# Moving weight sums out of the second down phase, and one operation for the last norm

## The chip, the cores and the metric

One core of a Trainium2 chip (trn2) runs the whole kernel. The metric is the device time of one execution in microseconds (us); smaller is better. TensorE (PE) multiplies, VectorE (DVE) and ScalarE (ACT) work on tiles element by element, GpSimd (POOL) and SyncE (SP) mostly issue DMA transfers.

## The reference, cut to what matters

```python
def swiglu(h, w_gate, w_up, w_down):
    return (jax.nn.silu(h @ w_gate) * (h @ w_up)) @ w_down

def reference(x, ...):                       # x: 1024 tokens x 1024 features, float32
    x = x + 0.5 * swiglu(rmsnorm(x, ffn1_norm), ffn1_w_gate, ffn1_w_up, ffn1_w_down)
    x = x + hybrid_mixer(rmsnorm(x, mix_norm), ...)
    x = x + 0.5 * swiglu(rmsnorm(x, ffn2_norm), ffn2_w_gate, ffn2_w_up, ffn2_w_down)
    return rmsnorm(x, final_norm)            # x / sqrt(mean(x*x) + eps) * final_norm
```

The hidden width is 2816, which is 22 blocks of 128 rows. The change concerns the second `swiglu` and the last `rmsnorm`.

## The kernel before

**Products.** Every float32 operand is cut into a rounded high part (`fp32r`, made by ACT, line 169) and the rest (DVE, line 170); a product is three matmuls, high by high, high by low, low by high. The large products go by a scheme of seven products on 2 x 2 blocks instead of eight: sums and differences of the blocks on either side are multiplied (P1, P2, P3, P5, P6, P7, Q4), and the seven results are added up into four output blocks. All matmuls are recorded on line 91.

**Phases.** `gate_up(i)` computes the hidden activations of FFN number i (0 for the first, 1 for the second), one hidden block m per unit, and `down(i)` multiplies them by the down weights. The mixer lies between `down(0)` and `gate_up(1)`. `down` runs sixteen turns over four output groups g (`TURNS`, line 376). A turn takes two or three row pairs q of the eleven (`NQ`): turn 0 two, turns 1 to 12 three, turns 13 to 15 two, so a turn is 42 or 63 matmuls. Turns 0 to 11 add their partial results in DRAM with an accumulating DMA (`Turn.add`, line 835, issued by POOL); turns 12 to 15 finish the outputs in SBUF (`Turn.end`, line 875) and call `ready`, which for i = 1 is `to_output`: sum of squares on ACT (line 1382), mean on DVE (1385, 1388), product with the weights `gb` of the norm on DVE (1390), the power -1/2 on POOL (1395), the product with it on DVE for one half (1399) and on ACT for the other (1401), and the store (1402).

**Where the sums of the down phase come from.** The two phases are built differently.
- In `down(0)` the stationary operand is made of the weights. `left` (line 460) takes four raw weight blocks from the prefetching loader `L` (two buffers, so loads run two turns ahead), makes three sums on DVE (lines 482, 484, 485) and splits seven operands. The moving operand is hidden activations: `Aside` made their sums during `gate_up(0)` and put all seven away in DRAM (`c_sp[0]`, line 644); `rights_back` (line 748) reads them back, four loads ahead.
- In `down(1)` the stationary operand is hidden activations. `Aside` put the seven sums away in `c_sp[1]`; `left_back` (line 503) reads them back straight into `w` tiles, each load issued just ahead of its split. The moving operand is weights: `rights_rows` (line 764) takes a 1 MB raw row pair from `L`, makes four sums on DVE (line 771) and splits seven operands.

**Order.** The tile framework keeps each engine's instructions in one queue, in an order that it works out when the kernel is built; a waiting instruction holds up those behind it. `MADE` and `UPTO` (lines 374, 375) say how many moving operands must be ready after each turn, in both phases. P1 and P2 of a turn share a PSUM bank, as do P7 and Q4, and P5 and P3: the second may start only when the first has been read out (lines 842 and 845 for P1, 858 for P7, 860 for P5). `s` tiles come from a pool of 72 buffers, `w` tiles from one of 10.

Of the kernel before, what the change touches and what calls it, by code (L numbers as in the profile page):

```python
# [10 lines left out]
F32 = mybir.dt.float32  # L11
# [6 lines left out]
P = 128  # L18
# [7 lines left out]
HALF = 512  # L26
# [15 lines left out]
def hybrid_block(ctx: ExitStack, tc: tile.TileContext, t: dict):  # L42
# [329 lines left out]


# [10 lines left out]
    def ffn_weights(i, pre, nstd):  # L384
# [6 lines left out]
        for j, (g, q0, q1) in enumerate(TURNS):  # L391
            if i:
                continue
            n = (q1 - q0) * P
            rows = wd[2 * q0 * P : 2 * q1 * P].rearrange("(k two p) c -> two p k c", two=2, p=P)
            yield [(b * n, n, (lambda a: a.rearrange("p (k c) -> p k c", c=P)),
                    rows[two, :, :, d * P : (d + 1) * P])
                   for b, (two, d) in enumerate(((1, g), (0, g), (1, g + 4), (0, g + 4)))]
        for q in range(NQ * i):
            yield [part(0, wd[2 * q * P : 2 * (q + 1) * P])]  # L400

# [101 lines left out]
    def left_back(g, q0, q1):  # L503

        a = {}
        n = (q1 - q0) * P

        def load(to, i):
            nc.sync.dma_start(out=to.rearrange("p (k c) -> p k c", c=P),
                              in_=c_sp[1][i, q0:q1, :, g * P : (g + 1) * P].rearrange("k p c -> p k c"))  # L510

        def begin(i):
            raw = w4(F32)[:, : 2 * n]
            for j in range(2):
                load(raw[:, j * n : (j + 1) * n], i + j)
            return raw

        yield a
        raw = begin(0)
        yield  # L520
        for i, after_it in ((0, 4), (4, 2), (2, 6)):
            now = raw
            if after_it < 6:
                raw = begin(after_it)
            else:
                raw = s()[:, :n]
                load(raw, 6)
            parts = split(w4()[:, : 2 * n], w4()[:, : 2 * n], now)
            for j in range(2):
                a[FACTORS[i + j]] = tuple(x[:, j * n : (j + 1) * n] for x in parts)  # L530
            yield
        a["Q4"] = split(s(F32R)[:, :n], s(F32R)[:, :n], raw)
        yield

# [97 lines left out]

    class Aside:

        def __init__(self, i):
            self.sp, self.op = c_sp[i], ALU.add if i else ALU.subtract
            self.names = (("P1", "P5", "P2", "P3", "P7", "P6", "Q4"), ("P1", "P7", "P2", "Q4", "P5", "P6", "P3"))[i]
            self.raw = 0, 2, 3, (1 if i else None)  # L640
            self.even = {}

        def put(self, j, i, x):
            nc.gpsimd.dma_start(out=self.sp[FACTORS.index(self.names[i]), j], in_=x)  # L644
# [4 lines left out]

        def take(self, m, hf, x):  # L650
            j, odd = divmod(m, 2)
            if not odd:
# [3 lines left out]
                else:  # L656
                    self.e1 = x
                    self.t1 = self.comb(s(), self.e0, x, self.op)
# [4 lines left out]
            else:  # L663
# [3 lines left out]
                t3 = self.comb(self.e1, x, self.e1, self.op)  # L667
                self.put(j, 4, t3)
                t4 = self.comb(s(), t2, self.o0, self.op)
# [5 lines left out]
    def gate_up(i, act, started, nstd):  # L675
# [50 lines left out]
        for m in range(nstd + 2, NF):  # L726
# [4 lines left out]
            else:  # L731
                prep = iter(())
                makers[i] = Prep(i)
                makers[i].begin(0)
            for n, name in enumerate(FEW):
                unit.do(name)
                next(prep, None)
                if i in makers:
                    makers[i].step()
                    makers[i].upto(UPTO[0] * (n + 1))  # L740
# [7 lines left out]
    def rights_back(ahead=4):  # L748
# [4 lines left out]
        def load():  # L753
            q, name = todo[len(raws)]
            raws.append(s())
            nc.sync.dma_start(out=raws[-1], in_=c_sp[0][FACTORS.index(name), q])
# [7 lines left out]
    def rights_rows():  # L764


        def done(name, x):
            b[name] = split(s(F32R), s(F32R), x)

        def comb(out, x, y, op):  # L770
            nc.vector.tensor_tensor(out=out, in0=x, in1=y, op=op)  # L771
            return out

        for q in range(NQ):
            b = ring[q] = {}
            raw, _ = L.take()
            b11, b12, b21, b22 = (raw[:, i * HALF : (i + 1) * HALF] for i in range(4))
            done("P1", b11)
            comb(b11, b11, b12, ALU.subtract)
            yield  # L780
            done("P7", comb(b12, b22, b12, ALU.subtract))
            yield
            done("P5", b11)
            yield
            done("P6", comb(b11, b11, b22, ALU.add))
            yield
            done("P2", b21)
            comb(b21, b11, b21, ALU.subtract)
            yield
            done("Q4", b21)  # L790
            yield
            done("P3", b22)
            L.load()
            yield

    class Prep:


        def __init__(self, i):
            self.i, self.made, self.lefts = i, 0, iter(())  # L800
            self.rights = rights_rows() if i else rights_back()
# [6 lines left out]
        def begin(self, j):  # L808
            if j < len(TURNS):
                g, q0, q1 = TURNS[j]  # L810
                self.lefts = left_back(g, q0, q1) if self.i else left(L.take()[0], (q1 - q0) * P, "P3")
# [564 lines left out]
    def to_output(tt, hf):  # L1376
# [13 lines left out]
        nc.vector.tensor_tensor(out=r, in0=r, in1=gb[hf], op=ALU.mult)  # L1390
# [5 lines left out]
        for hf in range(2):  # L1396
            r = rows[tt, hf]
            if hf:
                nc.vector.tensor_scalar(out=r, in0=r, scalar1=inv, scalar2=None, op0=ALU.mult)
            else:  # L1400
                nc.scalar.activation(r, r, AF.Identity, scale=inv)
# [29 lines left out]
```

## Time and profile before

| | us |
|---|---|
| median of 3 runs | 1896.9 (1896.22 to 1897.58) |
| the profiled execution | 1896.36 |
| its span, first to last instruction | 1894.7 |
| mean granted TensorE clock | 0.986 of full |

PE is busy for 97% of the span, DVE for 73%, ACT for 47%, POOL for 13%. The span is about: first `gate_up` to 476 us, `down(0)` to 689, mixer to about 1240, second `gate_up` to 1643, `down(1)` to 1886, then the last outputs. A time is read against PE: where PE is busy at full clock, other engines cost nothing; where it isn't, the rows say what it waited for.

### The profile page before, as it was taken

The numbers are of one execution on the slowest core, as the hardware profiler recorded it, in microseconds if no ns is written. First come the engines' busy times: TensorE is split into PE (matmuls) and PEld (weight loads), VectorE is DVE, ScalarE is ACT, GpSimd is POOL, SyncE is SP. The second block draws the span as 40 slices with busy tenths as digits, with TensorE's granted clock in tenths as the row PEclk, the third lists the DMA queues.
The fourth block names the chain that finished last, engine by engine and source line by source line (L and its number), as shares of the span: only waits on it lengthen the run. The fifth ranks groups of instructions, "written<-read, shape, count | busy, mean of one in ns | idle before, by whom it ended". The sixth has DMA issues, their size and how long they took to land.

```text
span 1894.7 us, 23205 instructions
## 1 busy us (share of the span) xinstructions
PE 1833.0 (97%) x8200; PEld 1508.1 (80%) x8200; DVE 1381.2 (73%) x2167; ACT 893.5 (47%) x1602; POOL 252.4 (13%) x400
## 2 busy tenths in 40 slices
PE   6999999999999999999999999999999999989997
PEld 5777888888888878888888878887888888777775
DVE  4788666666777797768787898658766666755768
ACT  3543222223555455667677775524322222344544
POOL 1201101010222221010101000210110101122211
PEclk8999999999999999999999999999999999999998
DMA  7213333334999853241313343412433333598985
GB/s 235 93 56 127 102 106 106 109 97 143 239 232 223 229 195 91 63 100 34 95 45 73 98 136 103 145 47 60 149 107 111 100 98 104 174 196 207 211 192 180
DMA packets 252933, 246.93 MB, mean 130 GB/s; under 512 B 14176, under 2 KB 197008, under 8 KB 252816
## 3 DMA queue, kind: packets, MB, share of 16 engines
q1 hardware_dynamic: 217072, 157.87, 27.8%
q0 software_dynamic: 35744, 87.58, 18.3%
q8 instruction: 64, 1.05, 0.2%
q14 instruction: 53, 0.43, 0.1%
HBM read 150.76 MB, written 85.20 MB: 125 GB/s over the span
## 4 chain that ended last, share of the span: by engine, by line
PE 68%; issue 15%; DVE 7%; DMA 4%; POOL 3%; ACT 1%; SPq 1%; POOLq 0%; DVEq 0%; ACTq 0%
PE ps L91 67%; DMA w<-c_sp 2%; DVE w L170 1%; DVE s L875 1%; POOL r_sp L835 1%; POOL c_sp L644 1%; DVE s L170 1%; DMA s<-c_sp 1%; DVE s L269 1%; PE ps L277 0%; DVE s L176 0%; POOL x_sp L835 0%; ACT w L169 0%; DMA r_sp<-s 0%; DMA raw<-in_ffn_w_gate 0%
## 5 line engine op out<-in xcount | busy, mean ns | idle before, releaser
L91 PE MATMUL ps<-s,w 128*128 128x512 f32 (+1 forms) x6400 | 1527.1, 393 | 38.6 <-ACT s L175 11.8
L91 PEld LDWEIGHTS ps<-s,w 128*128 128x128 f32 x6400 | 1198.2, 189 | 293.7 <-ACT s L175 12.7
L169 ACT CAST w<-raw 128x1024 fp32r<-128x1024 f32 (+2 forms) x158 | 157.5, 998 | 289.1 <-PE ps L91 189.1
L170 DVE TENSOR_TENSOR w<-raw,w 128x1024 fp32r<-128x1024 f32 (+2 forms) x158 | 182.0, 1153 | 109.4 <-PE ps L91 56.0
L91 PE MATMUL ps<-s,s 128*128 128x512 f32 (+3 forms) x944 | 241.4, 382 | 6.0 <-ACT s L858 4.3
L91 PEld LDWEIGHTS ps<-s,s 128*128 128x128 f32 x944 | 177.7, 189 | 46.1 <-ACT s L858 6.5
L644 POOL DMA_DIRECT2D c_sp<-s x154 | 83.5, 542 | 763.1 <-DVE s L630 579.8
L170 DVE TENSOR_TENSOR w<-w,w 128x768 fp32r<-128x768 f32 (+2 forms) x102 | 103.3, 1013 | 78.5 <-ACT w L169 39.3
L170 DVE TENSOR_TENSOR s<-s,s 128x512 fp32r<-128x512 f32 (+2 forms) x181 | 118.6, 670 | 39.8 <-ACT s L169 39.2
L169 ACT CAST w<-w 128x768 fp32r<-128x768 f32 (+2 forms) x102 | 89.6, 878 | 85.1 <-DMA w<-c_sp 39.3
L169 ACT CAST s<-s 128x512 fp32r<-128x512 f32 (+2 forms) x181 | 104.6, 607 | 43.4 <-DMA s<-c_sp 31.6
L626 ACT ACTIVATE s<-s 128x512 f32<-128x512 f32 x38 | 24.1, 633 | 190.0 <-DVE s L625 190.0
L170 DVE TENSOR_TENSOR s<-raw,s 128x512 fp32r<-128x512 f32 (+2 forms) x131 | 86.2, 666 | 25.9 <-ACT s L169 25.5
L482 DVE TENSOR_TENSOR w<-raw 128x1024 f32<-128x1024 f32 (+2 forms) x54 | 60.6, 1124 | 47.7 <-PE ps L91 46.7
L169 ACT CAST s<-raw 128x512 fp32r<-128x512 f32 (+2 forms) x131 | 76.7, 602 | 38.7 <-DVE raw L771 38.6
L611 ACT ACTIVATE s<-ps 128x512 f32<-128x512 f32 x38 | 22.7, 598 | 113.2 <-PE ps L91 113.2
L1254 DVE TENSOR_TENSOR s<-s,ps 128x128 f32<-128x128 f32 (+2 forms) x96 | 52.7, 548 | 16.8 <-ACT s L1250 16.4
L1242 ACT ACTIVATE s<-ps 128x128 f32<-128x128 f32 (+2 forms) x96 | 47.0, 490 | 37.7 <-PE ps L91 37.3
L835 POOL DMA_DIRECT2D r_sp<-s x48 | 41.6, 876 | 149.6 <-ACT s L854 48.3
L1250 ACT ACTIVATE s<-s 128x128 f32<-128x128 f32 (+2 forms) x96 | 50.2, 523 | 20.6 <-DVE s L1246 19.3
L617 DVE TENSOR_TENSOR s<-s,ps 128x512 f32<-128x512 f32 x38 | 26.0, 685 | 45.0 <-PE ps L91 45.0
L835 POOL DMA_DIRECT2D x_sp<-s x48 | 41.6, 866 | 126.3 <-DVE s L860 60.6
(133 smaller groups left out, 1697.6 us busy)
## 6 DMA issues: line engine op xcount, KB each, us to landing
c_sp<-s POOLq DMA_DIRECT2D x154, 256.0 KB, 2.5
raw<-in_ffn_w_gate SPq DMA_DIRECT2D x43, 512.0 KB, 3.9
raw<-in_ffn_w_up SPq DMA_DIRECT2D x43, 512.0 KB, 5.2
x_sp<-s POOLq DMA_DIRECT2D x80, 256.0 KB, 4.5
s<-c_sp SPq DMA_DIRECT2D x77, 256.0 KB, 7.1
r_sp<-s POOLq DMA_DIRECT2D x64, 256.0 KB, 5.1
w<-c_sp SPq DMA_DIRECT2D x72, 192.0 KB, 5.0
raw<-in_ffn_w_down SPq DMA_DIRECT2D x11, 1024.0 KB, 8.9
```

The costliest lines, as they stand in the source:

```text
L91: nc.tensor.matmul(out, lhs, rhs, **kw)
L169: nc.scalar.copy(hi, x)
L170: nc.vector.tensor_tensor(out=lo, in0=x, in1=f(hi), op=ALU.subtract)
L482: nc.vector.tensor_tensor(out=two(y), in0=two(blk(1, 2)), in1=blk(3).unsqueeze(1).to_broadcast([P, 2, n]), op=ALU.add)
L611: last_silu[0] = nc.scalar.activation(self.s0, o, AF.Silu)
L617: nc.vector.tensor_tensor(out=self.u3, in0=self.u2, in1=self.o[2], op=ALU.add)
L626: last_silu[0] = nc.scalar.activation(self.u2, self.u2, AF.Silu)
L644: nc.gpsimd.dma_start(out=self.sp[FACTORS.index(self.names[i]), j], in_=x)
L835: nc.gpsimd.dma_start(out=self.acc(self.g + 4 * i, hf), in_=x, accum_op=ALU.add)
L1242: behind(nc.scalar.activation(u["s"][:, cols], u["z"][:, cols], AF.Exp), table_set)
L1250: nc.scalar.activation(sc, sc, AF.Ln, bias=1.0)
L1254: nc.vector.tensor_tensor(out=sc, in0=sc, in1=u["z"][:, cols], op=ALU.max)
```

## The change

`down(1)` gets the form of `down(0)`. `Aside` for i = 1 no longer makes sums of the hidden activations: each hidden tile goes as it is to a new DRAM tensor `l_sp`, in four pieces per row, and the loader `L` reads four blocks of it per turn for `left`. During `gate_up(1)` one unit in most loads four half rows of the down weights through SP (`weights`), makes their four differences and sums on DVE (`differences`) and puts these four away in `c_sp[1]`; eleven of the units 5 to 19 do so, one row pair each. `rights_back` serves both phases; for i = 1 it reads P1, P2 and P3 straight from the weights. `left_back` and `rights_rows` go. In `to_output` the product with `gb` and the product with 1/rms become one `scalar_tensor_tensor` on DVE for each half.

```diff
+    l_sp = dr.tile([4, 4, P, NQ, P], F32, name="l_sp")
...
         for j, (g, q0, q1) in enumerate(TURNS):
+            n = (q1 - q0) * P
             if i:
+                yield [(b * n, n, (lambda a: a.rearrange("p (k c) -> p k c", c=P)), l_sp[b, g, :, q0:q1, :])
+                       for b in range(4)]
                 continue
...
-        for q in range(NQ * i):
-            yield [part(0, wd[2 * q * P : 2 * (q + 1) * P])]
...
-    def left_back(g, q0, q1):
...
+    wd2 = t["ffn2_w_down"][0]
+
     class Aside:
...
+        def weights(self, j):
+            if not self.part or j >= NQ:
+                return
+            self.w = [s() for _ in range(4)]
+            for i in range(4):
+                nc.sync.dma_start(out=self.w[i], in_=wd2[(2 * j + i // 2) * P : (2 * j + i // 2 + 1) * P, hs(i % 2)])
+
+        def differences(self, j):
+            if not self.part or j >= NQ:
+                return
+            b11, b12, b21, b22 = self.w
+            t1 = self.comb(b11, b11, b12, ALU.subtract)
+            self.put(j, 1, t1)
+            t3 = self.comb(b12, b22, b12, ALU.subtract)
+            self.put(j, 4, t3)
+            t2 = self.comb(b22, t1, b22, ALU.add)
+            self.put(j, 5, t2)
+            t4 = self.comb(b21, t2, b21, ALU.subtract)
+            self.put(j, 6, t4)
+
         def take(self, m, hf, x):
             j, odd = divmod(m, 2)
+            if self.part:
+                nc.gpsimd.dma_start(out=l_sp[2 * hf + 1 - odd, :, :, j, :].rearrange("g p c -> p g c"),
+                                    in_=x.rearrange("p (g c) -> p g c", c=P))
+                return
...
+            pair = (m - nstd - 2) * NQ // (NF - nstd - 4)
+            odd = pair == (m - nstd - 1) * NQ // (NF - nstd - 4)
             for n, name in enumerate(FEW):
                 unit.do(name)
                 next(prep, None)
+                if n == 0 and not odd:
+                    out.weights(pair)
+                if n == 5 and not odd:
+                    out.differences(pair)
...
-    def rights_back(ahead=4):
+    def rights_back(part, ahead=4):
...
-            nc.sync.dma_start(out=raws[-1], in_=c_sp[0][FACTORS.index(name), q])
+            src = c_sp[part][FACTORS.index(name), q]
+            if part and name in ("P1", "P2", "P3"):
+                m = 2 * q + int(name != "P1")
+                src = wd2[m * P : (m + 1) * P, hs(int(name == "P3"))]
+            nc.sync.dma_start(out=raws[-1], in_=src)
...
-    def rights_rows():
...
-            self.rights = rights_rows() if i else rights_back()
+            self.rights = rights_back(i)
...
-                self.lefts = left_back(g, q0, q1) if self.i else left(L.take()[0], (q1 - q0) * P, "P3")
+                self.lefts = left(L.take()[0], (q1 - q0) * P, "P3")
...
-        nc.vector.tensor_tensor(out=r, in0=r, in1=gb[hf], op=ALU.mult)
...
-            if hf:
-                nc.vector.tensor_scalar(out=r, in0=r, scalar1=inv, scalar2=None, op0=ALU.mult)
-            else:
-                nc.scalar.activation(r, r, AF.Identity, scale=inv)
+            nc.vector.scalar_tensor_tensor(out=r, in0=r, scalar=inv, in1=gb[hf], op0=ALU.mult, op1=ALU.mult)
```

## Rows read from the trace of the kernel before

**Rows 1.** The page: busy time of the engines, and DMA share in 40 slices.
```profile
PE 1833.0 (97%) x8200; PEld 1508.1 (80%) x8200; DVE 1381.2 (73%) x2167; ACT 893.5 (47%) x1602; POOL 252.4 (13%) x400
...
DMA  7213333334999853241313343412433333598985
```
**Rows 2.** Busy time by stretch: `down(1)` and its end, `down(0)` and its end, `gate_up(1)`.
```profile
core 0: us, PE busy (x) PEld busy (x) DVE busy (x) ACT busy (x) POOL busy (x), PEclk, DMA share, GB/s
1643.30:1844.36 201.06, 185.37 (x780) 148.38 (x779) 132.29 (x196) 99.07 (x170) 44.34 (x53) 0.97 0.86 204
1844.36:1886.40 42.04, 37.10 (x145) 28.72 (x143) 39.86 (x83) 19.13 (x46) 5.40 (x6) 0.92 0.64 196
476.30:654.30 178.00, 177.66 (x781) 146.12 (x780) 129.11 (x195) 98.93 (x170) 43.96 (x53) 1.00 0.94 232
654.30:689.30 35.00, 34.01 (x149) 27.51 (x147) 34.73 (x61) 12.87 (x22) 7.09 (x13) 1.00 0.64 210
1330.00:1630.00 300.00, 300.00 (x1325) 248.27 (x1325) 200.91 (x260) 84.48 (x114) 30.89 (x57) 1.00 0.35 113
```
**Rows 3.** PE in order of time (start, us, count): into `down(1)`, its last matmuls.
```profile
1640.60 10.36 PE L91 MATMUL ps<-s,w 128*128 128x512 f32 x45
...
1884.85 1.53 PE L91 MATMUL ps<-s,w 128*128 128x512 f32 x6
```
**Rows 4.** What PE waited for, 1625 to 1895 us: total, times, longest.
```profile
PE ps L91 <- DVE s L845: 9.2, 4, 4.0
PE ps L91 <- ACT w L169: 4.5, 2, 2.8
PE ps L91 <- ACT s L858: 4.3, 4, 1.8
```
**Rows 5.** Groups of instructions in `down(1)`, 1643.3 to 1844.4 us (columns as on the page).
```profile
L169 ACT CAST w<-w 128x768 fp32r<-128x768 f32 x36 | 30.0, 834 | 48.2 <-DMA w<-c_sp 37.9 <-DVE w L170 5.5 <-PE ps L91 4.2
L771 DVE TENSOR_TENSOR raw<-raw 128x512 f32<-128x512 f32 x38 | 26.2, 689 | 0.8
```
**Rows 6.** In order of time: one late load in `down(1)`.
```profile
1799.48 12.16 SPq L509 DMA_DIRECT2D w<-c_sp  x3
...
1808.89 0.83 ACT L169 CAST w<-w 128x768 fp32r<-128x768 f32 x1 [9.44 <-DMA w<-c_sp]
...
1811.37 0.68 DVE L845 TENSOR_TENSOR s<-s,ps 128x512 f32<-128x512 f32 x1
...
1812.10 3.84 PE L91 MATMUL ps<-s,w 128*128 128x512 f32 x9 [4.03 <-DVE s L845]
```
**Rows 7.** Groups of instructions in `down(0)`, 476.3 to 654.3 us.
```profile
L169 ACT CAST s<-s 128x512 fp32r<-128x512 f32 x65 | 39.9, 620 | 20.5 <-DMA s<-c_sp 20.4
L482 DVE TENSOR_TENSOR w<-raw 128x768 f32<-128x768 f32 x12 | 11.5, 955 | 8.4 <-PE ps L91 8.4
L484 DVE TENSOR_TENSOR raw<-w,raw 128x384 f32<-128x384 f32 x12 | 6.7, 558 | 0.3
```
**Rows 8.** DMA issues around `down(0)`, 455 to 680 us: count, size, median us to landing.
```profile
s<-c_sp SPq DMA_DIRECT2D x73, 256.0 KB, 7.4
```
**Rows 9.** Groups of instructions in `gate_up(1)`, 1330 to 1630 us.
```profile
L644 POOL DMA_DIRECT2D c_sp<-s x57 | 30.9, 542 | 268.4 <-DVE s L630 224.3 <-DVE s L647 40.1 <-issue 3.0
L630 DVE SCALAR_TENSOR_TENSOR s<-s,s 128x512 f32<-128x512 f32 x32 | 22.0, 688 | 0.6
L647 DVE TENSOR_TENSOR s<-s,s 128x512 f32<-128x512 f32 x32 | 20.7, 688 | 0.6
```
**Rows 10.** DVE groups from 1844.4 us to the end.
```profile
L1390 DVE TENSOR_TENSOR s<-s,s 128x512 f32<-128x512 f32 x16 | 10.9, 682 | 0.0
L1399 DVE TENSOR_SCALAR s<-s,sm 128x512 f32<-128x512 f32 x8 | 3.9, 484 | 2.2 <-POOL sm L1395 2.2
```
**Rows 11.** The last outputs in order of time.
```profile
1886.94 0.68 DVE L875 TENSOR_TENSOR s<-s,ps 128x512 f32<-128x512 f32 x1
...
1887.83 0.86 POOL L1395 TENSOR_TENSOR sm<-sm,mhalf 128x1 f32<-128x1 f32 x1 [7.52 <-DVE sm L1388]
...
1888.72 0.48 DVE L1399 TENSOR_SCALAR s<-s,sm 128x512 f32<-128x512 f32 x1 [0.44 <-POOL sm L1395]
...
1890.31 0.72 ACT L1401 ACTIVATE s<-s,sm 128x512 f32<-128x512 f32 x1 [0.87 <-POOL sm L1395]
```

More of the change, by code (lines that the diff above doesn't have):

```diff
@@ L391, in ffn_weights @@
         for j, (g, q0, q1) in enumerate(TURNS):
+            n = (q1 - q0) * P
             if i:
+                yield [(b * n, n, (lambda a: a.rearrange("p (k c) -> p k c", c=P)), l_sp[b, g, :, q0:q1, :])
+                       for b in range(4)]
                 continue
-            n = (q1 - q0) * P
             rows = wd[2 * q0 * P : 2 * q1 * P].rearrange("(k two p) c -> two p k c", two=2, p=P)
@@ L500, in left @@
         L.load()
-        yield
-    def left_back(g, q0, q1):
[L505 to L524, printed above, removed]
-            else:
[L526 to L532, printed above, removed]
         yield
@@ L631, in store @@
             self.out(hf, u)
+    wd2 = t["ffn2_w_down"][0]
     class Aside:
         def __init__(self, i):
[L638 to L641, printed above, removed]
+            self.part = i
+            self.names = ("P1", "P5", "P2", "P3", "P7", "P6", "Q4")
         def put(self, j, i, x):
-            nc.gpsimd.dma_start(out=self.sp[FACTORS.index(self.names[i]), j], in_=x)
+            nc.gpsimd.dma_start(out=c_sp[self.part][FACTORS.index(self.names[i]), j], in_=x)
         def comb(self, out, x, y, op):
@@ L657, in take @@
                     self.e1 = x
-                    self.t1 = self.comb(s(), self.e0, x, self.op)
+                    self.t1 = self.comb(s(), self.e0, x, ALU.subtract)
                     self.put(j, 1, self.t1)
@@ L666, in take @@
                 self.put(j, 5, t2)
-                t3 = self.comb(self.e1, x, self.e1, self.op)
+                t3 = self.comb(self.e1, x, self.e1, ALU.subtract)
                 self.put(j, 4, t3)
-                t4 = self.comb(s(), t2, self.o0, self.op)
+                t4 = self.comb(s(), t2, self.o0, ALU.subtract)
                 self.put(j, 6, t4)
@@ L762, in rights_back @@
             yield
-    def rights_rows():
[L767 to L794, printed above, removed]
     class Prep:
@@ L1397, in to_output @@
             r = rows[tt, hf]
-            if hf:
-                nc.vector.tensor_scalar(out=r, in0=r, scalar1=inv, scalar2=None, op0=ALU.mult)
-            else:
-                nc.scalar.activation(r, r, AF.Identity, scale=inv)
+            nc.vector.scalar_tensor_tensor(out=r, in0=r, scalar=inv, in1=gb[hf], op0=ALU.mult, op1=ALU.mult)
             nc.sync.dma_start(out=out[tt * P : (tt + 1) * P, hs(hf)], in_=r)
```

## The prediction
> **What bounds the kernel now.** I read the page first: PE is busy for 97% of the span [rows 1], so nothing that other engines save counts unless PE stands still or runs slow somewhere. Second, the busy time by stretch, which compares the two down phases over the same work [rows 2]. `gate_up(1)` gives the price of a matmul without any wait: 1325 in 300.00 us, 0.2264 us each. In `down(0)`, from its first matmul to the last Q4 that belongs to a three-pair turn, 781 matmuls take 178.00 us where the price makes 176.8: 1.2 us lost. The same stretch of `down(1)` has 780 and takes 201.06 us where 176.6 would do: 24.5 us lost, 15.7 of them with PE idle, the rest at a lower granted clock (0.97 in the mean against 1.00) and in the pipeline's refills. The reader is to see two rows with equal counts and unequal lengths. (`down(1)` begins 12 matmuls of the last unit, 2.7 us, after the first of rows 3, hence 1643.3.) The remaining turns: 145 matmuls in 42.04 us, 32.8 by price, 9.2 lost; in `down(0)` 149 in 35.00, 33.7 by price, 1.3 lost [rows 2].
>
> Third, the waits of PE: DVE line 845, ACT line 169 and ACT line 858 hold most [rows 4]. Two of the three read a PSUM bank out; neither is slow work, so the question is what they stood behind. Fourth, the groups: in `down(1)` ACT stands idle 37.9 us for `w<-c_sp`, the loads of `left_back` [rows 5]. Fifth, one such place in order of time: the load is issued at 1799.48, ACT waits 9.44 us for it with the read-outs queued behind, DVE's line 845 comes at 1811.37, and PE idles 4.03 us [rows 6]. So `down(1)` loses its time to left operands that are fetched just ahead of use. It is not DMA capacity: the DMA share is 0.86 at 204 GB/s there, and 0.94 at 232 GB/s in `down(0)`, which loses nothing [rows 2]. In `down(0)` ACT also waits for its loads (20.4 us for `s<-c_sp`), but these run four ahead, and PE doesn't feel it [rows 7].
>
> **The change part by part.** *Left operands of `down(1)`.* The seven just-in-time loads per turn go; four raw blocks come through `L`, two turns (some 28 us) ahead. The wait of rows 5 goes, and with it the chain of rows 6. What is late next is the right operand, now loaded from DRAM with four loads in flight. `down(0)` splits 65 such tiles in 178 us, one per 2.7 us [rows 7]; a load lands 7.4 us after its issue [rows 8], so four in flight deliver one per 1.85 us. The queue of SP is in order, and in the new form it carries what it carries in `down(0)`: 64 blocks and 77 tiles, plus the outputs at the end. The bytes are those of before (eleven row pairs seven times over on one side, four on the other, with the sides exchanged), in longer runs for the left blocks (up to 1536 bytes in place of 512). I take the length of `down(0)`: 201.06 - 178.00 = 23.1 us gained; bounds: 24.5 (nothing lost any more) and 12 (the right operands bring back half of it).
>
> *DVE in `down(1)`.* Removed: the sums of line 771, 38 in the stretch, 26.2 us [rows 5]. Added: `left`'s three sums a turn, in the stretch some 11.5 + 6.7 + 6.7 = 24.9 us by `down(0)` [rows 7], line 485 having the shape of 484. Equal, and DVE was busy for 132.29 of 201.06 us [rows 2]. Zero.
>
> *`gate_up(1)`.* DVE gives up four sums of hidden tiles per row pair and gets four of weights. They lie closer together: 44 in units 5 to 19 in place of 32 in that stretch [rows 9], 12 x 0.69 = 8.3 us more, beside 99 us in which DVE is idle there while PE never is [rows 2]. POOL: 44 hidden tiles in pieces and 44 sums in place of 77 tiles. The trace of before has no store in such pieces. From below it costs the 0.542 us of a whole tile [rows 9], from above four times that, 2.17 us, if POOL pays by the piece; 44 x 2.17 + 44 x 0.542 = 119 us at most in some 370, where POOL is busy about a tenth. Zero on the path either way. SP gets 44 loads of 256 KB ahead of the raw loads; a raw load is used more than one unit (19 us) after its issue, and DMA is busy for 0.35 there [rows 2]. Covered; if the cover went, see the third rival. The waits that are added are the four sums at the end of a unit, on the loads issued at its beginning; behind them on DVE stand that unit's last read-outs and the next unit's splits.
>
> *Last turns and `to_output`.* Here DVE is the limit: 39.86 of 42.04 us busy [rows 2]. Removed from it: 16 products at 0.682 = 10.9 us and 8 at 0.484 = 3.9 us; added 16 fused ones, priced by line 630, which is such an operation, at 0.688 = 11.0 us [rows 9, 10]. Net -3.8 us; ACT loses its 8. Also added: `left`'s sums for turns 13 to 15, made one turn earlier, one of 512 and two of 256 elements each, 0.68 + 2 x 0.43 (estimated from 0.558 at 384 and 0.682 at 512 [rows 7, 10]) = 1.5 us, three times 4.6. Net +0.8 us, of which turn 12 with its 63 matmuls can hide a third. Then the wait for POOL's power: before, the product with `gb` stood in its shadow, and DVE idled only 2.2 us in eight waits [rows 10]; now up to 8 x 0.68 = 5.5 us more stand open unless other work is put there. Bounds for the four turns -3.8 and +6; I take +1.5, near the net sum, since the read-outs of the next turn are there to fill the gap.
>
> The Trainium skill, "VectorE: DVE Perf Modes", section "The perf-mode tier table", says that a float32 operation in SBUF with one tensor source runs at twice the rate of one with two. The rows agree (0.484 against 0.682), so by that rule the fused operation pays the full rate for both halves and takes one half over from ACT; the gain of 3.8 us above is all that is left of removing sixteen operations.
>
> *Behind the last matmul.* It ends at 1886.4 [rows 3], the span 8.3 us later. DVE reaches the last read-out at 1886.94 because a product with `gb` stood before it; that is 0.6 us at most to be gained. Then power, two fused products on DVE (1.3 us) where DVE and ACT took 0.48 and 0.72 side by side [rows 11], twice in order: -0.3 to +1.4. I take +0.5.
>
> Sum: -23.1 + 0 + 0 + 1.5 + 0.5 = -21.1 us. On the profiled execution: 1896.36 - 21.1 = 1875.3. The median lies 0.5 us above it, so the forecast is 1875.8.
>
> **Rivals.**
> *The end costs more.* Every wait for the power stays open, +6 instead of +1.5, and the tail takes +1.4: 1875.8 + 5.4 = 1881. For it: the four waits on line 845, of which part lie in the last turns, and DVE's 95% there [rows 2, 4]. Against: the order of DVE is worked out anew.
>
> *Half the gain.* The right operands stall PE now and then, since `down(1)` also loads `r_sp` and the norm's weights and its pool holds two more tiles than `down(0)`: 23.1 becomes 12, 1887. Against: a rate of one load per 1.85 us where 2.7 is asked [rows 7, 8].
>
> *No change.* The right loads become what the left loads were. This sets in where a load takes longer than 4 x 2.7 = 10.8 us to land, against 7.4 measured: the 23.1 us stay lost, and with the 2.0 of the end and the tail the time is 1899. The Trainium skill, "DMA: Bandwidth & Descriptors", speaks for it: its section "Anatomy of one DMA" puts a fixed 2.0 us on each DMA, and its rule under "Bandwidth" asks for batches of 1 MiB or more, while the change replaces eleven of 1 MB by 77 of 256 KB. By its fit 77 loads one after another take an estimated 200 us, about what the stretch takes now. `down(0)` runs 73 such loads at 232 GB/s without a stall, which speaks against it.
>
> *Slower: the sums of the weights stop DVE in `gate_up(1)`.* Place: the four sums in eleven units. If their loads come late, because SP waits for four free `s` buffers beside the 56 that the norm's operands hold, DVE stands before the read-outs of the unit, and PE waits for the bank. Price: four sums wholly exposed, 4 x 0.688 = 2.75 us, in eleven units 30 us: 1906. It decides from 21.1 / 11 = 1.9 us per unit on. Against: a third of DVE's time is free there and no PE wait of any length stands in that stretch [rows 2]; by my count of live tiles 13 of the 16 free buffers are used.
>
> *Better.* The gain reaches 24.5 and the end goes by its lower bounds (-3.8 and -0.3): 1896.9 - 28.6 = 1868.
>
> **How the numbers follow.** Forecast 0.62 (own range 1871 to 1880), end costs more 0.12, half the gain 0.12, better 0.04, no change 0.05, slower 0.05. The predicted time is the forecast's, 1875.8. The range runs from 1868 to 1888: it takes in the better case, the costlier end and the middle of the half gain, and leaves out no change and slower. Within 0.2% (3.8 us), about what a measurement of this kernel can tell from no change, lies only the fourth rival: faster 0.90, same 0.05, slower 0.05.
>
> **What would show it.** In the profile after, the stretch from the first matmul of `down(1)` to the Q4 of turn 12 should take 178 to 180 us with PE idle for under 2, at a granted clock of 1.00, with no ACT wait on a load of left blocks, and with waits of ACT on `s<-c_sp` that PE doesn't feel. `gate_up(1)` should still show PE busy for 300 of 300 us. The last 145 matmuls should take 41 to 46 us, with DVE waiting longer for POOL's line 1395 than 2.2 us. I am wrong if PE waits for lines 169 or 170 on `s` tiles in `down(1)`, if a unit of `gate_up(1)` grows by a microsecond or more, or if DVE's queue in the last turns loses more than 6 us.

## The result, and the profile after

| | before | after |
|---|---|---|
| median of the runs (us) | 1896.99 (1896.22 to 1897.58) | 1871.79 (1869.02 to 1873.51, 4 runs) |
| ratio, 95% interval | | 0.9867 (0.9856 to 0.9879) |
| the profiled execution; its span | 1896.36; 1894.7 | 1872.05; 1870.0 |
| mean granted TensorE clock | 0.986 | 0.989 |

25.2 us less, where 21.1 were forecast. Three stretches of the kernel after, cut as in [rows 2] (same columns), the second now from the Q4 of turn 12 to the very end:

```profile
1643.70:1820.90 177.20, 177.20 (x781) 146.27 (x780) 126.92 (x191) 97.42 (x168) 42.46 (x50) 1.00 0.94 231
1820.90:1870.00 49.10, 34.56 (x145) 26.36 (x143) 42.14 (x85) 15.51 (x41) 4.75 (x8) 0.93 0.45 147
1330.00:1630.00 300.00, 300.00 (x1325) 248.42 (x1324) 206.28 (x268) 85.88 (x116) 48.25 (x77) 1.00 0.51 166
```

The same cut to the end, in the kernel before:

```profile
1844.36:1894.70 50.34, 37.10 (x145) 28.72 (x143) 43.39 (x90) 22.01 (x51) 7.18 (x8) 0.89 0.59 185
```

`down(1)` up to turn 12 went from 201.06 us [rows 2] to 177.20: -23.9, with PE busy all the time at a granted clock of 1.00. The end went from 50.34 to 49.10: -1.2. `down(1)` starts 0.4 us later (1643.7 against 1643.3). Together -24.7, the difference of the spans. The middle of the kernel stayed as it was: PE is busy for 300 of 300 us in `gate_up(1)`.

What PE waited for, 1625 to 1880 us (total, times, longest), of after. The lines have moved: 482 is now 483, 845 is 817, 875 is 847, 1395 is 1366, and 1369 is the fused operation.

```profile
PE ps L91 <- DVE s L847: 3.2, 4, 1.6
PE ps L91 <- DVE s L817: 1.0, 1, 1.0
```

The 9.2 us behind line 845 and the 4.5 behind ACT's line 169 [rows 4] are gone; what is left lies in the last turns. The groups of `down(1)` that answer to [rows 5] and [rows 7]:

```profile
L169 ACT CAST s<-s 128x512 fp32r<-128x512 f32 x65 | 39.9, 619 | 24.1 <-DMA s<-in_ffn_w_down 18.4 <-DMA s<-c_sp 5.4
...
L483 DVE TENSOR_TENSOR w<-raw 128x768 f32<-128x768 f32 x12 | 11.5, 954 | 8.5 <-PE ps L91 8.5
```

ACT still waits 24 us for loads, now of right operands. These run four ahead, and PE doesn't feel it, as in `down(0)`.

### The profile page after: what moved, and what is told of

Same layout as the page of the kernel before. It is cut to its first block, busy times and chain, and to the rows that moved or that the text cites. A ratio compares the mean times of both kernels' runs of the same rounds, so it can differ in the third digit from the quotient of the medians.

```text
span 1870.0 us, 23392 instructions
## 1 busy us (share of the span) xinstructions
PE 1821.4 (97%) x8200; PEld 1504.2 (80%) x8200; DVE 1377.7 (74%) x2163; ACT 887.0 (47%) x1594; POOL 264.6 (14%) x411
## 4 chain that ended last, share of the span: by engine, by line
PE 89%; DVE 5%; DMA 2%; issue 2%; ACT 1%; SPq 1%; POOL 0%; DVEq 0%; POOLq 0%; ACTq 0%
PE ps L91 87%; DVE s L847 1%; DVE w L170 1%; DVE s L269 1%; PE ps L277 0%; DVE s L176 0%; DMA raw<-in_ffn_w_gate 0%; DMA s<-c_sp 0%; PE ps L1072 0%; DVE s L1369 0%; DVE s L170 0%; DMA s<-in_x 0%; ACT w L169 0%; SPq L896 0%; DMA s<-in_ffn_w_down 0%
## 5 line engine op out<-in xcount | busy, mean ns | idle before, releaser
L91 PE MATMUL ps<-s,w 128*128 128x512 f32 (+1 forms) x6400 | 1519.1, 392 | 25.1 <-ACT s L175 12.6
L169 ACT CAST w<-raw 128x1024 fp32r<-128x1024 f32 (+2 forms) x190 | 182.3, 961 | 310.5 <-PE ps L91 222.6
L170 DVE TENSOR_TENSOR w<-raw,w 128x1024 fp32r<-128x1024 f32 (+2 forms) x190 | 210.2, 1107 | 103.4 <-ACT w L169 62.3
L170 DVE TENSOR_TENSOR s<-s,s 128x512 fp32r<-128x512 f32 x242 | 162.9, 685 | 53.9 <-ACT s L169 53.2
L169 ACT CAST s<-s 128x512 fp32r<-128x512 f32 x242 | 143.3, 618 | 57.7 <-DMA s<-c_sp 27.1
L614 POOL DMA_DIRECT2D c_sp<-s x121 | 65.7, 543 | 419.3 <-DVE s L599 288.5
L483 DVE TENSOR_TENSOR w<-raw 128x1024 f32<-128x1024 f32 (+2 forms) x70 | 74.8, 1070 | 57.9 <-PE ps L91 51.4
L170 DVE TENSOR_TENSOR w<-w,w 128x1024 fp32r<-128x1024 f32 (+2 forms) x70 | 74.9, 1070 | 51.8 <-PE ps L91 40.9
L169 ACT CAST w<-w 128x1024 fp32r<-128x1024 f32 (+2 forms) x70 | 64.8, 925 | 49.0 <-DVE w L483 40.0
L643 POOL DMA_DIRECT2D l_sp<-s x44 | 33.2, 755 | 324.5 <-DVE s L599 263.0
L617 DVE TENSOR_TENSOR s<-s,s 128x512 f32<-128x512 f32 x88 | 58.7, 688 | 1.3
```

What stands on the lines that cost most here:

```text
L91: nc.tensor.matmul(out, lhs, rhs, **kw)
L169: nc.scalar.copy(hi, x)
L170: nc.vector.tensor_tensor(out=lo, in0=x, in1=f(hi), op=ALU.subtract)
L483: nc.vector.tensor_tensor(out=two(y), in0=two(blk(1, 2)), in1=blk(3).unsqueeze(1).to_broadcast([P, 2, n]), op=ALU.add)
L614: nc.gpsimd.dma_start(out=c_sp[self.part][FACTORS.index(self.names[i]), j], in_=x)
L643: nc.gpsimd.dma_start(out=l_sp[2 * hf + 1 - odd, :, :, j, :].rearrange("g p c -> p g c"), in_=x.rearrange("p (g c) -> p g c", c=P))
```

## The experiments

A stretch is cut from the first matmul of `down(1)` to the Q4 of turn 12 in each kernel. Its loss is its length less the price of its matmuls (0.2264 us each, from the prediction). Stretches are compared rather than spans, since `down(1)` begins anywhere from 1640 to 1648 us in these runs whatever the kernel. A stretch comes from one execution, a median from four to ten; the ratio is to the executions of before that ran beside it.

| run | built on | median us | ratio to before (95%) | stretch us | loss us |
|---|---|---|---|---|---|
| before | | 1896 to 1898 | 1 | 201.06 | 24.5 |
| form | after | 1874.09 | 0.9885 (0.9858 to 0.9912) | 177.63 | 0.8 |
| out | before | 1896.03 | 0.9994 (0.9980 to 1.0009) | 200.91 | 24.1 |
| early | before | 1893.59 | 0.9982 (0.9967 to 0.9997) | 198.43 | 22.5 |
| late | after | 1869.51 | 0.9859 (0.9837 to 0.9882) | 176.83 | 0.0 |
| stile | before | 1908.90 | 1.0057 (1.0034 to 1.0079) | 208.64 | 32.9 |
| pieces | after | 1872.61 | 0.9863 (0.9841 to 0.9885) | | |
| double | after | 1872.65 | 0.9862 (0.9834 to 0.9890) | | |
| pool | after | 1871.92 | 0.9863 (0.9840 to 0.9886) | | |
| quarters | before | 1897.76 | 1.0000 (0.9988 to 1.0013) | 201.66 | 25.1 |
| noload | before | 1880.61 | 0.9917 (0.9897 to 0.9937) | 187.35 | 10.5 |
| two | after | 1922.82 | 1.0137 (1.0117 to 1.0156) | | 48 in 200 us |
| noacc | before | 1873.50 | 0.9882 (0.9866 to 0.9899) | 179.70 | 3.1 |

**The two parts alone.** *form* is the kernel after with the old last norm, *out* the kernel before with the new one:

```diff
     # out
-        nc.vector.tensor_tensor(out=r, in0=r, in1=gb[hf], op=ALU.mult)
...
+            nc.vector.scalar_tensor_tensor(out=r, in0=r, scalar=inv, in1=gb[hf], op0=ALU.mult, op1=ALU.mult)
```

> The new form of the down phase, with the last norm's operations as before (product with the weights, then the scaling, half on DVE and half on ACT). Theory (the left operands of the second down phase came too late): the stretch up to turn 12's Q4 stays at 177 us, and the time is 1871 to 1876, since the end has 3 us more of DVE work. Rival (the fused operation is what brings a good part, since DVE limits the last turns): 1878 or more.

> The kernel before, with the fused operation of the last norm alone. Theory (late left operands): the stretch stays at 201 us, and the time at 1894 to 1899. Rival (fused operation): 1890 or less.

*form*, the stretch and the end (columns of rows 2):

```profile
1647.00:1824.63 177.63, 177.63 (x781) 146.06 (x780) 127.31 (x192) 97.47 (x168) 42.43 (x50) 1.00 0.94 231
...
1824.63:1874.30 49.67, 35.81 (x145) 27.32 (x143) 43.46 (x92) 21.26 (x49) 7.17 (x8) 0.90 0.44 145
```

*out*, its end:

```profile
1848.31:1896.80 48.49, 34.04 (x145) 26.30 (x143) 41.81 (x82) 15.93 (x43) 5.20 (x8) 0.91 0.61 191
```

The form brings 22 us, by the medians 1896.22 to 1874.09. The fused operation shortens the end by 1.9 us in the old form (50.34 to 48.49) and by 0.6 in the new (49.67 to 49.10); in the time *out* can't be told from before, and *form* lies 2.3 us above after, inside the intervals.

**Is it how far ahead the left loads are issued?** The prediction says that the old form loses its time to loads "fetched just ahead of use". *early* puts each pair of left loads of the old form one product earlier in the program. *late* puts the left blocks of the new form later, to the beginning of their turn's preparation.

```diff
     # early
+        raws = [begin(0)]
         yield a
-        raw = begin(0)
+        raws.append(begin(4))
         yield
-        for i, after_it in ((0, 4), (4, 2), (2, 6)):
+        for i, after_it in ((0, 2), (4, 6), (2, None)):
...
     # late
-        L.load()
+        if ahead:
+            L.load()
...
+                if self.i and j > 1:
+                    L.load()
```

> The kernel before, in which each load of a pair of left operands is issued one product earlier (two pairs in flight in place of one); same transfers, same sums. Theory (late left operands): ACT's wait of 37.9 us for these loads falls by a third to two thirds and 5 to 20 us of the 24.5 come back: 1877 to 1892. Rival (runs of 512 bytes make the transfers too slow in total, so that an earlier issue doesn't help): 1895 to 1899.

> The kernel after, in which the four left blocks of turns 2 to 15 are loaded when their preparation begins, not two turns ahead. Theory (late left operands): ACT stands before the first split of every turn for about the 5 us of a landing, less the product in between, some 3 us, and PE loses 3 to 20 us: 1875 to 1892. Rival (the gain is due to the moved sums or to fewer packets): 1870 to 1874.

*early* gains 2.6 us by the medians, and its stretch loses 22.5 us in place of 24.5: less than its theory and more than its rival. ACT's wait for the loads didn't fall (41.8 us). (Its trace is the slowest of its ten executions, 1897.81 us.) Why so little stands in SP's queue, 1640 to 1845 us (total, times, longest). Before:

```profile
SPq L509 <- PE ps L91: 41.6, 14, 7.4
SPq L509 <- DVE w L170: 35.3, 17, 3.8
SPq L509 <- DMA w<-c_sp: 32.9, 11, 7.8
```

*early*:

```profile
SPq L509 <- PE ps L91: 61.1, 18, 12.3
SPq L509 <- DVE w L170: 18.8, 10, 4.1
SPq L509 <- DMA w<-c_sp: 3.4, 3, 1.9
```

SP already stands before line 509, since the loads go into `w` tiles, of which there are ten, and PE or DVE must first be done with the tile. A load moved forward in the program waits as long for its tile as before (behind PE and DVE together 79.9 us against 76.9). The third row fell from 32.9 to 3.4 us; before, it was mostly the third pair of a turn standing behind the landing, and then the split, of the first. The lead can be read from the issue times of the traces: from the issue of a pair's second load until ACT is free for its split, 6.3 us in the mean in *out*, whose `down(1)` is that of before, and 7.3 in *early*. So the move bought one microsecond. *late* did not test what it was meant to: its loader line waits for its buffer about as long as that of after, 99.0 us in 13 waits against 109.8 in 13, so the loads still go out as soon as a raw buffer is free. Its time can't be told from that of after.

**Other buffers.** *stile* loads the left operands of the old form into `s` tiles, of which there are 72, to take the wait for `w` tiles away.

```diff
-        def begin(i):
-            raw = w4(F32)[:, : 2 * n]
-            for j in range(2):
-                load(raw[:, j * n : (j + 1) * n], i + j)
+        def begin(i, m=2):
+            raw = [s()[:, :n] for _ in range(m)]
+            for j in range(m):
+                load(raw[j], i + j)
             return raw
...
```

> The kernel before, with the raw left operands of the second down phase loaded into single s tiles in place of pairs in w tiles; the order of the program, the transfers and their 512-byte runs stay, and each pair takes two splits of half the length (some 0.16 us of DVE and 0.2 us of ACT more for each). New theory (the loads of the old form are issued late because their w buffers, ten in all, come free only when PE has finished with older operands): SP's waits for PE in front of these loads mostly go, ACT's wait for w<-c_sp with them, and 12 to 24 us come back: 1872 to 1884. Rivals (the 512-byte runs, or SP's order of issue, make the loads late): 1893 to 1899.

It became slower, by 11 us, where 12 to 24 us of gain were expected. SP's waits, 1640 to 1860 us:

```profile
SPq L509 <- DMA r_sp<-s: 18.6, 4, 7.9
...
SPq L509 <- PE ps L91: 13.2, 19, 1.9
```

The wait for PE fell from 41.6 to 13.2 us, but now the loads wait for `s` tiles whose partial results POOL's store has not yet read, up to 7.9 us. The `s` pool ran short, one scarce buffer was exchanged for another, and this run neither supports nor refutes the theory.

**Is it the size of the transfers?** Two runs. *pieces* reads `l_sp` in runs of 512 bytes in place of up to 1536. *quarters* replaces, in the old form, each 1 MB load of weights by four of 256 KB, issued apart from each other.

```diff
     # pieces
-    l_sp = dr.tile([4, 4, P, NQ, P], F32, name="l_sp")
+    l_sp = dr.tile([4, 4, NQ, P, P], F32, name="l_sp")
...
     # quarters
+            def refill(i):
+                if q + 2 < NQ:
+                    m = 2 * (q + 2) + i // 2
+                    nc.sync.dma_start(out=raw[:, i * HALF : (i + 1) * HALF], in_=wd2[m * P : (m + 1) * P, hs(i % 2)])
...
```

> The kernel after, with the put-aside hidden tiles laid out so that a left block is read in runs of 512 bytes, as in the old form, not up to 1536. Theory (buffers): no change, 1869 to 1875. Rival (longer runs are what made the left loads arrive in time): 1878 to 1892.

> The kernel before, in which the down weights of row pairs 2 to 10 come not as one load of 1 MB each but as four of 256 KB, each issued where its quarter of the buffer is read for the last time; same bytes, same two buffers, left operands as before. Theory now (a 1 MB load goes ahead of the left operands on SP's queue, and these land 9 us after issue in place of 5): ACT's wait for w<-c_sp falls to less than half of 37.9 us and 10 to 22 us come back: 1875 to 1887. Rival (the w buffers alone, which come free late): 1893 to 1899.

Neither moves the time. *pieces* is 0.8 us above after, inside both intervals; *quarters* is at 1.0000, with a loss of 25.1 us. ACT's waits in *quarters*, 1640 to 1845 us:

```profile
ACT w L169 <- DMA w<-c_sp: 34.8, 13, 7.5
ACT s L169 <- DMA s<-c_sp: 21.9, 8, 6.3
```

The longest wait fell from 9.4 to 7.5 us, the total of both kinds rose. Cutting the bursts of 1 MB up does not help; the same bytes still go through the same queue.

**Is it the amount of traffic?** *noload* leaves nine of the eleven weight loads of the old `down(1)` out (built on *quarters*), *noacc* the 48 accumulating stores of its turns 0 to 11. Both keep the order of the left loads.

```diff
     # noload
-                if q + 2 < NQ:
+                if q + 2 < 2:
...
     # noacc
-            nc.gpsimd.dma_start(out=self.acc(self.g + 4 * i, hf), in_=x, accum_op=ALU.add)
+            if not self.skip:
+                nc.gpsimd.dma_start(out=self.acc(self.g + 4 * i, hf), in_=x, accum_op=ALU.add)
```

> The kernel before without nine of the eleven loads of the down weights in the second down phase: row pairs 2 to 10 are computed from what the two buffers hold, so the products are those of other weights. All sums, splits, products and left loads stay. Theory (loads of the weights ahead of the left operands): the second down phase loses under 8 us in place of 24.5, 1872 to 1881. Rival (w buffers that come free late): the loss stays, 1892 to 1898.

> The kernel before without the 48 accumulating stores of the second down phase (12.6 MB of some 41 MB there, on POOL's queue): the partial results of turns 0 to 11 are computed and not added. Left loads, weight loads, buffers and SP's order stay. Theory (the phase asks for nearly all that the DMA engines can move, and the old form leaves them idle for a seventh of the time because its loads wait for buffers, so any traffic less helps): the stretch of 201 us falls to 177 to 190, as in the run without weight loads, 1872 to 1884. Rival (the left loads stand behind the weight loads on SP's own queue, and POOL's traffic is nothing to them): 195 us or more, 1891 to 1898.

The stretch of *noload*, then that of *noacc* (columns of rows 2):

```profile
1640.30:1827.65 187.35, 180.93 (x781) 147.47 (x779) 133.83 (x197) 100.33 (x171) 44.23 (x53) 0.98 0.81 173
```

```profile
1648.40:1828.10 179.70, 178.12 (x780) 145.70 (x780) 134.84 (x200) 100.47 (x171) 2.70 (x5) 1.00 0.53 166
```

And the left loads: count, size, median us from issue to landing, of before, *noload* and *noacc* in turn (1640 to 1845 us, *noacc* 1643 to 1835):

```profile
w<-c_sp SPq DMA_DIRECT2D x68, 192.0 KB, 5.2
```

```profile
w<-c_sp SPq DMA_DIRECT2D x68, 192.0 KB, 4.5
```

```profile
w<-c_sp SPq DMA_DIRECT2D x71, 192.0 KB, 3.2
```

ACT's wait for these loads, 37.9 us before [rows 5], in *noload* and in *noacc* (the same windows):

```profile
ACT w L169 <- DMA w<-c_sp: 11.8, 5, 3.2
```

```profile
ACT w L169 <- DMA w<-c_sp: 5.2, 6, 1.6
```

As the landing time falls from 5.2 over 4.5 to 3.2 us, ACT's wait falls from 37.9 over 11.8 to 5.2 and the loss from 24.5 over 10.5 to 3.1. (The medians are those of the loads whose landing the trace knows, fewer than 20 of some 70. With the full traffic they are 5.2, 5.4, 4.9 and 5.0 in before, *out*, *early* and *quarters*, so 3.2 stands clear of the scatter and 4.5 hardly; the waits and losses do.) What SP waits for stays: in *noload* line 509 even waits 100.5 us for PE. One might think that *noload* wins because SP no longer stands before the weight loads, but the left loads don't go out earlier: by the measure used for *early* their lead is 5.3 us in *noload* and 5.1 in *noacc*, not longer than the 6.3 of *out*. So the old form loses time where a short lead meets a landing time that other traffic stretches. That shorter landing cures it is shown (*noacc*, 23 us by the medians). *form* gains the same 22 us at the full traffic, by taking these loads off the path; which part of it does that, the longer lead or fewer loads that wait for each other, is not separated. One reservation: *noacc* also frees `s` tiles sooner, as no store reads them any more; *noload* doesn't have that and saves 14 of the 24.5. *noacc* came out as its theory had it; *noload* did in time, but its loss is above the 8 us that were expected.

**How far ahead must the right loads of the new form run?** *two* gives them two fixed buffers, so two in flight in place of four.

```diff
+        fixed = [s() for _ in range(2)] if part else []
...
-            raws.append(s())
+            raws.append(fixed[len(raws) % 2] if part else s())
...
-            while len(raws) < min(len(todo), i + ahead):
+            while len(raws) < min(len(todo), i + (2 if part else ahead)):
```

> The kernel after, in which the right operands of the second down phase are loaded into two fixed buffers, so two loads in flight in place of four. At 7.4 to 7.8 us to landing two in flight deliver one per 3.8 us, plus the split, where PE asks for one per 2.7. Theory (four in flight are needed to keep ahead): 60 to 90 us more, 1930 to 1960. Rival (a load lands sooner when fewer are in flight, and the lead that the prepared operands have hides the rest): under 20 us more, 1870 to 1890.

25 us slower than before, so some 50 more than after; less than the 60 to 90 that were expected. SP's wait for the two buffers in *two*, then its loads, then those of after (1640 to 1845 us):

```profile
SPq L761 <- DVE s L170: 77.2, 51, 5.5
```

```profile
s<-c_sp SPq DMA_DIRECT2D x35, 256.0 KB, 3.2
...
s<-in_ffn_w_down SPq DMA_DIRECT2D x25, 256.0 KB, 4.8
```

```profile
s<-c_sp SPq DMA_DIRECT2D x37, 256.0 KB, 7.8
raw<-l_sp SPq DMA_DIRECT2D x40, 192.0 KB, 5.9
s<-in_ffn_w_down SPq DMA_DIRECT2D x28, 256.0 KB, 7.9
```

With two in flight a load lands in 3.2 to 4.8 us, with four in 7.8. A good part of the landing time of [rows 8] thus goes with the other loads in flight (and with the rest of the traffic: the DMA share is 0.77 from 1650 to 1850 us in *two*), and a landing time read with four in flight is too long for two. By the prediction's rule (in flight times 2.7 us against the landing time) two would just have done: 5.4 against 3.2 to 4.8. The rule leaves out that a buffer is also held until its split is done: SP waits 77 us for line 170, the second half of the split, in 51 waits. So the number in flight, with the buffers that it needs, decides: this is the "no change" rival brought about, and it costs twice what the change brought.

**Does DVE in `gate_up(1)` matter?** *double* makes four more differences in each of the eleven units.

```diff
             self.put(j, 6, t4)
+            for _ in range(4):
+                self.comb(s(), t4, t2, ALU.subtract)
```

> The kernel after, with four more DVE operations of 128x512 after the four sums of the weights in each of the eleven units of the second gate_up (44 more, some 30 us of DVE; their results are not used). Theory (these sums lie in DVE's idle time): no change, 1869 to 1875, PE busy for 300 of 300 us in the stretch 1330 to 1630. Rival (the sums stop DVE before read-outs that PE waits for): 10 to 30 us more, 1882 to 1902.

```profile
1330.00:1630.00 300.00, 300.00 (x1325) 248.51 (x1324) 233.51 (x316) 85.90 (x113) 48.70 (x77) 1.00 0.51 165
```

DVE was busy for 27.2 us more (206.28 to 233.51), PE stayed at 300 of 300, and the time is that of after. DVE has room to spare there. The condition of the "slower" rival, loads that come late, was not brought about; in after PE is never idle in this stretch, so it didn't arise.

**Can the end be relieved?** *pool* gives the product with `gb` of one half to POOL, and its scaling to ACT.

```diff
+        if not hf:
+            nc.gpsimd.tensor_tensor(out=r, in0=r, in1=gb[hf], op=ALU.mult)
```

> The kernel after, with the norm's product for one half of each row tile made by POOL before the root is known and the scaling of that half by ACT; the other half keeps the fused DVE operation. Theory (DVE's queue limits the last turns): eight operations of 0.75 us leave DVE, the last 145 matmuls and what follows them take 49 us less 2 to 5: 1867 to 1870. Rival (POOL's product delays the power behind it on POOL, or slows DVE): 1872 to 1880.

No gain, where 2 to 5 us were expected: 1871.92 against 1871.79. POOL and DVE in the last turns of *pool*, from 1820 us (groups as on the page):

```profile
L1363 POOL TENSOR_TENSOR s<-s,s 128x512 f32<-128x512 f32 x8 | 10.6, 1332 | 26.9 <-ACT s L1354 26.9
```

```profile
L1372 DVE SCALAR_TENSOR_TENSOR s<-s,sm,s 128x512 f32<-128x512 f32 x8 | 6.0, 752 | 3.7 <-POOL sm L1368 3.4
...
L170 DVE TENSOR_TENSOR s<-raw,s 128x256 fp32r<-128x256 f32 x3 | 3.4, 1119 | 0.0
...
L483 DVE TENSOR_TENSOR w<-raw 128x512 f32<-128x512 f32 x2 | 2.5, 1228 | 0.0
```

Eight products left DVE, but five other operations of DVE that read two operands in SBUF took 1.12 and 1.23 us in the mean in place of 0.41 and 0.68, and the waits for the power grew from 2.6 to 3.4 us, though only eight operations wait for it in place of sixteen.

None of these versions beats after by more than its interval.

## Why the prediction was right, step by step

**`down(1)`: right in size, right in its remedy, wrong in part of its diagnosis.** -23.1 was forecast, -23.9 measured, and *form* shows that this part alone does it. The sign named for it is there: PE busy throughout, clock 1.00, ACT's waits on loads without an effect. The size was read off `down(0)`, which runs the same form, so it doesn't depend on the diagnosis; that three points of the diagnosis failed didn't cost it anything.

First, "It is not DMA capacity" holds for the bytes (after moves them at a share of 0.94 without a loss) and fails as a dismissal of the traffic. The argument compared DMA shares [rows 2] and didn't ask how long a load takes under them: *noacc* keeps the old order, takes traffic away and loses 3.1 us. And *early* shows that the moment of issue isn't set by the place in the program alone: SP waits for the tile. Whether more `w` tiles alone would have done was not tried.

Second, the place of [rows 6] was misread. The load that ACT waits for was not issued at 1799.48. SP's issues there, before, and the landing times of line 509's loads from 1760 to 1815 us:

```profile
1795.73 0.37 SPq L191 DMA_DIRECT2D raw<-in_ffn_w_down  x1
1796.15 6.63 SPq L509 DMA_DIRECT2D w<-c_sp  x4
```

```profile
DMA to landing us min/median/max: 7.3/9.2/12.2
```

The pair went out at 1796.15 and 1796.70, right behind 1 MB of weights, and landed some 12 us later, just before ACT's split at 1808.89. ACT had been free for it 2.7 us after the second issue. So the lead was short, but at the median landing of 5.2 us ACT would have waited 2.5 us and not 9.44.

Third, the lead of the new form is not two turns, some 28 us. A raw buffer comes free only with the last split of its turn, and a turn's splits are made a turn ahead of its products, so less than one of the two turns lies before them. SP's loads of one turn and ACT's first split of them, after:

```profile
1722.98 1.86 SPq L191 DMA_DIRECT2D raw<-l_sp  x4
```

```profile
1734.96 0.84 ACT L169 CAST w<-raw 128x768 fp32r<-128x768 f32 x1 [3.06 <-PE ps L91]
```

In turns 2 to 15 the last of the four loads goes out 6 to 13 us before that split, against a landing of 5.9. That was enough: ACT waits for PE there and for no left block.

The 24.5 us themselves are 15.7 of idle PE and 8.8 of longer busy time (185.37 against 176.6); how the 8.8 divide between the lower clock and refills no run shows.

**DVE in `down(1)`: zero, right.** 126.92 us busy in after, under PE all the time.

**`gate_up(1)`: zero, right.** The unknown price, the store in pieces, lies between its bounds of 0.542 and 2.17 us. Groups of after, 1330 to 1630 us:

```profile
L617 DVE TENSOR_TENSOR s<-s,s 128x512 f32<-128x512 f32 x44 | 30.3, 688 | 0.8
L643 POOL DMA_DIRECT2D l_sp<-s x33 | 24.9, 755 | 202.0 <-DVE s L599 196.8 <-issue 5.2
L614 POOL DMA_DIRECT2D c_sp<-s x44 | 24.1, 547 | 50.3 <-DVE s L617 46.4 <-issue 3.9
```

Four times the pieces cost 0.755 us on POOL in place of 0.542, far from four times. DVE got 5.4 us more (200.91 to 206.28) where 8.3 were estimated.

**Last turns and tail: the sign was wrong.** +1.5 and +0.5 were forecast, -1.2 measured; this term makes 3.2 of the 4.0 us by which the median undercut the forecast, and the stretch of `down(1)` the next 0.8. Up to the last matmul the stretch took 38.80 us in place of 42.04, so -3.2, near the lower bound of -3.8 and below the 41 to 46 us named as a sign; behind it 10.3 in place of 8.3, so +2.0, outside the bound of +1.4. That stretch of after:

```profile
1820.90:1859.70 38.80, 34.54 (x145) 26.36 (x143) 36.46 (x73) 12.79 (x33) 3.67 (x6) 1.00 0.49 159
```

The forecast took DVE's queue for the whole price and had no term for PE's clock. The 145 matmuls kept PE busy for 37.10 us before, at a granted clock of 0.92 [rows 2], that is in part at the lower of its two levels, and for 34.54 after at 1.00, the full level: 2.6 of the 3.2 us. PE's idle time fell by the other 0.7. It goes with the fused operation, in the one trace of each: up to its last matmul *out* took 36.79 us at 1.00, *form* 39.42 at 0.96. DVE of after, 1820.9 us to the end:

```profile
L1369 DVE SCALAR_TENSOR_TENSOR s<-s,sm,s 128x512 f32<-128x512 f32 x16 | 11.3, 748 | 2.9 <-POOL sm L1366 2.6
...
L485 DVE TENSOR_TENSOR raw<-w,raw 128x256 f32<-128x256 f32 x2 | 0.8, 420 | 0.0
```

DVE's own terms were mis-sized too: its load to the very end fell by 1.3 us (43.39 to 42.14), where +0.8 was worked out. The fused operation takes 0.748 us, not 0.688: line 630, which priced it [rows 9], has a constant where this one has a value for each partition; that this is the reason was not tested. Only two of the three turns' sums of `left` lie here (3.0 us, not 4.6). Seven splits of 512 columns on line 170 lie here where before there were ten (2.1 us less), which no term had. DVE waits 2.6 us for the power, 0.4 more than before, where up to 5.5 more were feared: the read-outs of the next turn fill the gap, as the forecast took it. The rule of the Trainium skill beside this sum ("VectorE: DVE Perf Modes", "The perf-mode tier table"), that one tensor source runs at twice the rate of two, is borne out only in direction: 0.484 against 0.682 us is a ratio of 1.4, not 2.

The tail in order of time, after:

```profile
1858.06 1.66 PE L91 MATMUL ps<-s,w 128*128 128x512 f32 x6 [0.44 <-DVE s L847]
...
1861.64 0.68 DVE L847 TENSOR_TENSOR s<-s,ps 128x512 f32<-128x512 f32 x1
...
1862.69 0.54 POOL L1366 TENSOR_TENSOR sm<-sm,mhalf 128x1 f32<-128x1 f32 x1 [6.73 <-DVE sm L1360]
...
1863.26 1.41 DVE L1369 SCALAR_TENSOR_TENSOR s<-s,sm,s 128x512 f32<-128x512 f32 x2 [0.65 <-POOL sm L1366]
...
1865.47 1.41 DVE L1369 SCALAR_TENSOR_TENSOR s<-s,sm,s 128x512 f32<-128x512 f32 x2 [0.72 <-POOL sm L1366]
```

The forecast saw the products in order (1.41 us for two). It did not see that PE, which finishes its turns sooner now, leaves more of DVE's work behind it: the last read-out starts 1.9 us after the last matmul's end (1859.72), before it was 0.6 [rows 3, 11]. Part of what the last turns gain is only moved behind the last matmul, so the two are to be costed as one term.

**The rivals.** "No change" did not come at four in flight, and *two* shows that its rule was too kind: the landing time grows with the number in flight, and the split holds the buffer too. The Trainium skill's rule of batches of 1 MiB or more ("DMA: Bandwidth & Descriptors", "Bandwidth") decides nothing here. It stands there, like the fit that made 200 us of these loads, beside transfers issued from GpSimd, while these are issued by SP; and by the runs 77 loads of 256 KB in after leave PE no wait in `down(1)`, and *quarters*, which cuts batches of 1 MB into quarters, moves nothing. "Half the gain" and "the end costs more" didn't come. The result lies halfway between the forecast (1875.8) and "better" (1868). (The prediction exchanges two numbers: "the third rival" beside `gate_up(1)` is "slower", and "the fourth", within 0.2%, is "no change".)

## What to carry to other kernels

A stall on a load is the difference of two times: how long before its use the load can be issued, for which a free buffer can matter more than the place in the program, and how long it takes to land under the traffic of that stage. Read both from the rows (the queue's own waits, the landing time of the very load that was waited for) before naming either as the cause; a DMA share below that of a stage that runs well doesn't clear the traffic. Where the same work already runs without loss elsewhere in the kernel, its stretch was here a better price for the change than the sum of operations was for the end. And where PE waits now and then, read its granted clock beside its idle time: the last turns gained 2.6 us by the clock and 0.7 by the waits.

## What the runs showed of the hardware

**A small operation of POOL depends on what DVE does beside it.** The power over 128x1 in the last turns, before and after:

```profile
L1395 POOL TENSOR_TENSOR sm<-sm,mhalf 128x1 f32<-128x1 f32 x8 | 7.2, 898 | 39.8 <-DVE sm L1388 39.8
```

```profile
L1366 POOL TENSOR_TENSOR sm<-sm,mhalf 128x1 f32<-128x1 f32 x8 | 4.8, 594 | 44.5 <-DVE sm L1360 44.5
```

Before, the product with `gb`, two operands in SBUF, ran on DVE beside it, as here ahead of the power at 1887.83 [rows 11]:

```profile
1887.60 0.68 DVE L1390 TENSOR_TENSOR s<-s,s 128x512 f32<-128x512 f32 x1
```

The power took 0.898 us; after, 0.594 in the mean, and 0.54 in the tail above, where DVE waits. It goes with the norm and not with the form of `down(1)`: 0.896 in *form*, 0.650 in *out*. In *pool* both sides slowed. The Trainium skill, "SBUF — State Buffer", section "Who interferes with whom", says that a DVE instruction with two SBUF inputs contends with a GpSimd instruction that reads SBUF; these rows agree. So the fused operation also saved 0.3 us of each power (0.25 in *out*), which no term of the prediction had.

**Landing time follows the traffic, not the DMA share alone.** The 192 KB load of the old form landed in 5.2, 4.5 or 3.2 us as the stage's DMA share was 0.86, 0.81 or 0.53, and a 256 KB load in 3.2 to 4.8 or 7.8 us with two or four in flight. But the 192 KB blocks of the new form landed in 5.9 us in after and 4.5 in *form* at the same share of 0.94. And a single load can stand far off the median: the pair of [rows 6] took 12 us, in a stage whose median is 5.2.
